# A hybrid decoder step: sample states streamed past C in four column groups, squares added ahead of their sums, diagonals in two instructions, the sample's list kept on the chip

## The chip, the cores and the metric

The kernel runs on one core of one Trainium2 chip. The metric is the device time of one execution in microseconds (us). A core has five engines that run at the same time, each through its own instructions in order: TensorE (PE in the profile, its weight loads PEld), VectorE (DVE), ScalarE (ACT), GpSimd (POOL) and SyncE (SP), whose queue issues most of the DMA transfers. They wait for one another by semaphores. TensorE reads SBUF and writes PSUM; the kernel takes PSUM in banks of 128 partitions x 512 f32 numbers.

## The reference, cut to what matters

One layer of a decoder step for 512 prompt tokens and 32 sample tokens (8 sequences of 4): a SwiGLU block, a mixing block with two parallel branches, attention over a memory, a second SwiGLU block. The change touches three places in the mixing block.

The state branch (SSD) has 8 groups of 4 heads, 64 channels a head, 128 state numbers a channel. For a group, `bm` and `cm` are its B and C (128 numbers a token), `xs` its input, and for the sample each sequence has a state `h0` of its own:

```
y_off = einsum('bctgn,bcgrpn->bctgrp', cc, h_in) * exp(a_cs)     # state times C
y = y_diag + y_off + d_skip * xs ;  y = y * silu(z)
yg = y by groups of 256 ;  yg = yg * rsqrt(mean(yg*yg) + EPS)     # norm of each group
```

The attention branch of the sample picks 256 of 4100 keys for each of the 32 tokens and attends to them alone:

```
score = sum over heads of wi * relu(qi . ki) ;  sel = top_k(score, 256)
phys = page_table[sel // 128] ; off = sel % 128      # keys and values come from paged pools,
                                                     # the last 4 positions are the new tokens
```

## The kernel before, in words

Activations lie transposed: features on partitions, 544 tokens (512 and 32) along the row. Each weight is split into a high and a low part (`wh`, made by ScalarE in L270, and `wl`, by VectorE in L271), each activation too (`uh`, `ul`), and the projections add three f32r products in L302; that line makes up most of TensorE's work. Weights come through SP's queue (L267) in pieces of 512 KB, with three raw and two split buffers.

Python generators issue the program. `weave` runs several at once: each yields an estimate of TensorE's time and of a delay, and `weave` takes the next one that is due. A scheduler of the language then orders each engine's instructions by its own estimate of when they are ready, so that an engine's order in the trace is near the order of issue but not the same; it also puts in all waits. A tile with a `tag` shares its buffers (`bufs`) with the other tiles of the tag, and a new tile waits until the old one's last reader is done.

In `ssd` two chains are woven with a third one as filler. `tails` runs `ssd_y` for the groups 0 to 7 one after another. The other chain is the sample's: the rest of `sample_lists`, then `sample_select`, then `sample_att`. The filler `fronts` runs the projections of the groups (`ssd_x`, `ssd_z`), up to two groups ahead of the tails, and when both are through the attention branch's output projection.

`ssd_y(g)`: the prompt's part is in chunks of 128 tokens (`pcb`, `pxt`, `pst`, later `pYo`, `pY`). For the sample, `turned(n)` transposes four sequences' states of two heads (L1395) and ScalarE copies them to `hT` (L1397, two buffers). Then four matmuls (L1409) each take one sequence's transposed state, 128x128, as the stationary operand and move that sequence's four columns of C (`XS[3]`) past it. This happens four times a group; results gather in the bank `pys`. L1414 adds the part of the new tokens to that bank, and L1417 (`pns`) makes the new states, which VectorE adds up (L1421) and SP stores (L1424). The decay E (L1439, one buffer) comes from DRAM in two halves (L1441) and multiplies the prompt's state part (L1454). `y` is formed for each of the group's two tiles, ScalarE squares it into `zts[i]` (L1463), and `rms` sums the squares over partitions: the squares are the stationary operand and a column of ones moves (L333), for both tiles and five blocks of tokens. After `rsqrt`, `rms` spreads the result over partitions: for each of the five blocks VectorE multiplies the identity by a column (L344, `dg`, two buffers) and TensorE multiplies ones by it (L345).

The sample's list: four partitions hold the four segments of a token's keys. `sample_lists` finds the threshold by bisection, numbers the selected keys of each segment by a running sum, and `max_index` (L1096) looks up the positions of the numbers 1 to 256 in each segment's own list. `sample_select` turns positions into rows of the pools (L1507 to L1517), counts which of the four new tokens are chosen (L1522), writes the four segment lists to DRAM (L1527), and reads them back shifted by the number of keys in the segments before (L1540), so that VectorE can put them together (L1544 to L1548). Two transposes and a copy give `slot` (L1552, L1553), the row numbers with which GpSimd gathers keys and values (L1591).

`sample_att` works in four steps of eight tokens. It spreads the queries into `qz` (16 small copies, L1601), adds two masks into the score bank `psS`: one (L1609) takes `lt`, which VectorE makes from the identity (L1608), and the list's mask `mk`, the other (L1610) takes `En`, loaded by SP (L1604, one buffer), and `bn`. Then the gathered keys are transposed (L1619), scored (L1626), and after the softmax the values are multiplied (L1663): 32 columns of weights are the stationary operand and 128 columns of values move, four of these matmuls going to the four 32-partition quarters of the bank `pO`.

Of the kernel before, what the change touches and what calls it, by code (L numbers as in the profile page):

```python
# [17 lines left out]
P = 128  # L18
# [12 lines left out]
def consts():  # L31
# [41 lines left out]
    less = seg[:, None] < a(4)[None]  # L73
    start = ((p // 4 * 16 + p % 4)[:, None] + a(4)[None] * 4) * 256
    c["c_ix2"] = f(np.concatenate([nm, same, Pre, it256, onb, onq, less, start], 1))
# [7 lines left out]
    c["c_att"] = f(np.concatenate([hm, En.reshape(P, 512)], 1))  # L83
# [85 lines left out]
class Net:  # L169
# [155 lines left out]
    def rms(self, sqs, inv_n, pool):  # L325
# [14 lines left out]
        yield 0.3, 4.0  # L340
        ps = self.ps1("psr")
# [366 lines left out]
    def mix(self, lead):  # L708
# [7 lines left out]
        self.mk = mx.tile([32, 256], F32, name="mk")  # L716
# [317 lines left out]
    def sample_lists(self):  # L1034
# [3 lines left out]
        ct = sp.tile([P, 560], F32, name="ct")  # L1038
        nc.sync.dma_start(ct, I["c_ix2"][:, 4:])
        cx = self.cx = views(ct, (("Blk", P), ("Pre", P), ("it256", 256), ("onb", 8), ("onq", 32), ("less", 4), ("start", 4)))  # L1040
        bits = sp.tile([P, 16, 3], U32, name="bits")
        nc.sync.dma_start(bits.rearrange("p a b -> p (a b)"), I["c_bits"])
        w = sp.tile([P, 24], F32, name="selw")
# [48 lines left out]
        nc.vector.scalar_tensor_tensor(A, S, n, A, op0=ALU.is_le, op1=ALU.mult)  # L1092
        nc.vector.tensor_tensor_scan(S, A, G, 0.0, op0=ALU.add, op1=ALU.add)
        yield 0.0, 3.0
        for r in range(32):
            nc.vector.max_index(self.IX[:, r * 8:(r + 1) * 8], cx["it256"][:, r * 8:(r + 1) * 8], S)  # L1096
            yield 0.0, 2.6
# [119 lines left out]
    def ssd(self, sel_ex, rounds):  # L1217
# [4 lines left out]
        self.fr, self.zt = {}, {}  # L1222
        fs = Flag()
# [83 lines left out]
    def ssd_y(self, g, z):  # L1307
# [65 lines left out]
        yield 0.5, 5.0  # L1373

# [12 lines left out]

        yield 0.0, 2.0
        ys = self.ps1("pys")
# [10 lines left out]
        turned(0)  # L1400
        yield 0.45, 0.8
        for n in range(4):
            i, q = n // 2, n % 2
            if n < 3:
                turned(n + 1)
                yield 0.45, 0.8
# [3 lines left out]
            yield 0.1  # L1410
# [24 lines left out]
        sqs = []  # L1435
        Y = []
        for i in range(2):
# [26 lines left out]
            sqs.append(zts[i])  # L1464
            Y.append(y)
        yield 0.0, 8.0
# [25 lines left out]
    def sample_select(self):  # L1492
        nc, I = self.nc, self.I
        IX, cx, c = self.IX, self.cx, self.cnt
        ex = ExitStack()
        sp = self.pool("sel", ex)
        dum = sp.tile([P, 256], F32, name="dum")

# [4 lines left out]
        nc.vector.tensor_scalar(ptf, ptb, 128.0, None, op0=ALU.mult)  # L1503
        pgi = sp.tile([P, 256], U32, name="pgi")
# [11 lines left out]
        nc.vector.tensor_scalar(dum, pgf, 8.0, 65536.0, op0=ALU.is_equal, op1=ALU.mult)  # L1516
        nc.vector.tensor_tensor(row, row, dum, op=ALU.add)  # L1517
        sel = sp.tile([P, 256], F32, name="selm")
        nc.vector.tensor_scalar(sel, cx["it256"], c, None, op0=ALU.is_le)
        fl = sp.tile([P, 4], F32, name="fl")  # L1520
        for j in range(4):
            nc.vector.scalar_tensor_tensor(dum, row, 65536.0 + j, sel, op0=ALU.is_equal, op1=ALU.mult, accum_out=fl[:, j:j + 1])  # L1522
        bn = self.bn
# [27 lines left out]
        for hf in range(2):  # L1551
            nc.tensor.transpose(ps[:, hf * 32:(hf + 1) * 32], R[:, 1, hf * P:(hf + 1) * P], self.ident[:32, :32])  # L1552
# [506 lines left out]
```

## Time and profile before

| what | value |
|---|---|
| median of 3 runs | 2251.27 us (2251.18 to 2252.69) |
| profiled execution, its own time | 2257.89 us |
| its span | 2256.1 us |
| mean granted TensorE clock over the span | 0.976 |
| TensorE busy | 2135.5 us, 95% |
| VectorE busy | 1336.8 us, 59% |
| ScalarE busy | 937.7 us, 42% |
| GpSimd busy | 475.9 us, 21% |

Busy time is the time in which an engine had at least one instruction of its own under way. Matmuls overlap in the pipeline, so a record's own length is more than what it costs; the distance from one start to the next tells that better. The granted clock has two levels in these records, 1.00 (2.4 GHz) and 0.50 (1.2 GHz). Each f32 matmul leaves two records, each f32r matmul one.

### The profile page before, as it was taken

The numbers are of one execution on the slowest core, as the hardware profiler recorded it, in microseconds if no ns is written. First come the engines' busy times: TensorE is split into PE (matmuls) and PEld (weight loads), VectorE is DVE, ScalarE is ACT, GpSimd is POOL, SyncE is SP. The second block draws the span as 40 slices with busy tenths as digits, with TensorE's granted clock in tenths as the row PEclk, the third lists the DMA queues.
The fourth block names the chain that finished last, engine by engine and source line by source line (L and its number), as shares of the span: only waits on it lengthen the run. The fifth ranks groups of instructions, "written<-read, shape, count | busy, mean of one in ns | idle before, by whom it ended". The sixth has DMA issues, their size and how long they took to land.

```text
span 2256.1 us, 41414 instructions
## 1 busy us (share of the span) xinstructions
PE 2135.5 (95%) x16769; PEld 2000.0 (89%) x16769; DVE 1336.8 (59%) x2801; ACT 937.7 (42%) x1717; POOL 475.9 (21%) x553
## 2 busy tenths in 40 slices
PE   7999999998999999879999999999999979999998
PEld 7999999997787689878888899999897879999998
DVE  6543333484778898885676578554664385423445
ACT  6323354355436664343444345232435253222233
POOL 0000010142132212245654531012420140000012
PEclk9999999999999999998999999999999999999999
DMA  6324564457432243255465454473444434232243
GB/s 204 113 80 141 164 214 164 128 133 228 143 94 84 72 114 113 70 159 146 140 178 152 121 145 153 139 226 99 161 150 143 171 99 131 79 99 87 87 122 104
DMA packets 319803, 301.72 MB, mean 134 GB/s; under 512 B 25432, under 2 KB 290264, under 8 KB 318564
## 3 DMA queue, kind: packets, MB, share of 16 engines
q1 hardware_dynamic: 310076, 272.45, 39.6%
q0 software_dynamic: 8576, 25.31, 3.7%
q8 instruction: 132, 2.16, 0.4%
q10 hardware_dynamic: 960, 1.31, 0.2%
q14 instruction: 59, 0.48, 0.1%
HBM read 261.01 MB, written 37.48 MB: 132 GB/s over the span
## 4 chain that ended last, share of the span: by engine, by line
PE 70%; DVE 14%; ACT 5%; POOL 4%; DMA 4%; issue 4%; SPq 0%; another core or an unknown queue 0%; DVEq 0%; POOLq 0%; ACTq 0%
PE pg L302 40%; PE pgh L302 14%; PE pmo L580 2%; DVE wl L271 2%; ACT wh L270 2%; DVE gtm L1065 1%; DVE XO L1297 1%; POOL kv L1591 1%; PE pys L1409 1%; DVE eqm L1096 1%; DMA wr<-in_ffn_wu 1%; POOL hT L375 1%; DMA yt<-yssd_d 1%; PE pmo L1852 1%; PE pkT L1619 1%
## 5 line engine op out<-in xcount | busy, mean ns | idle before, releaser
L270 ACT CAST wh<-wr 128x1024 fp32r<-128x1024 f32 (+3 forms) x362 | 341.0, 958 | 506.5 <-PE pg L302 278.6
L302 PE MATMUL pg<-uh,wh 128*128 128x256 f32 (+1 forms) x2336 | 506.7, 298 | 3.3 <-ACT CB L1285 1.5
L271 DVE TENSOR_TENSOR wl<-wr,wh 128x1024 fp32r<-128x1024 f32 (+3 forms) x338 | 390.2, 1167 | 199.4 <-ACT wh L270 191.1
L302 PE MATMUL pg<-uh,wl 128*128 128x256 f32 (+1 forms) x2336 | 496.0, 293 | 5.7 <-DVE wl L271 5.7
L302 PE MATMUL pg<-ul,wh 128*128 128x256 f32 (+1 forms) x2336 | 495.1, 293 | 0.0
L302 PEld LDWEIGHTS pg<-uh,wh 128*128 128x128 f32 x2336 | 383.1, 192 | 23.2 <-issue 16.7
L302 PEld LDWEIGHTS pg<-uh,wl 128*128 128x128 f32 x2336 | 382.5, 192 | 8.6 <-DVE wl L271 6.2
L302 PEld LDWEIGHTS pg<-ul,wh 128*128 128x128 f32 x2336 | 383.1, 192 | 2.9 <-issue 2.1
L302 PE MATMUL pgh<-uh,wl 128*128 128x256 f32 (+1 forms) x880 | 258.3, 296 | 12.2 <-DVE wl L271 11.8
L302 PE MATMUL pgh<-uh,wh 128*128 128x256 f32 (+2 forms) x880 | 260.9, 299 | 6.7 <-ACT wh L270 4.6
L302 PE MATMUL pgh<-ul,wh 128*128 128x256 f32 (+2 forms) x880 | 257.5, 294 | 1.9 <-POOL ul L311 1.2
L302 PEld LDWEIGHTS pgh<-uh,wl 128*128 128x128 f32 x880 | 168.5, 192 | 16.7 <-DVE wl L271 15.3
L302 PEld LDWEIGHTS pgh<-uh,wh 128*128 128x128 f32 (+1 forms) x880 | 170.0, 194 | 10.6 <-ACT wh L270 5.5
L302 PEld LDWEIGHTS pgh<-ul,wh 128*128 128x128 f32 (+1 forms) x880 | 170.7, 194 | 4.3 <-POOL ul L311 1.6
L359 POOL TENSOR_TENSOR sqf<-sqf,sqt 128x256 f32<-128x256 f32 (+1 forms) x52 | 55.8, 1073 | 516.7 <-ACT sqt L358 516.6
L302 PE MATMUL pgh<-hh,wh 128*128 128x288 f32 (+1 forms) x352 | 101.7, 289 | 0.0
L302 PE MATMUL pgh<-hh,wl 128*128 128x288 f32 (+1 forms) x352 | 100.9, 287 | 0.0
L302 PE MATMUL pgh<-hl,wh 128*128 128x288 f32 (+1 forms) x352 | 100.9, 287 | 0.0
L691 POOL DMA_INDIRECT G<-in_cache_kidx,ix x16 | 16.4, 1027 | 361.6 <-DVE ix L686 280.2
L1297 DVE SCALAR_TENSOR_TENSOR XO<-CB,convw,XO 128x600 f32<-128x600 f32 x96 | 80.3, 837 | 18.3 <-ACT XO L1295 17.8
L606 DVE TENSOR_TENSOR g<-pg,rt 128x544 f32<-128x544 f32 x32 | 23.2, 725 | 102.2 <-PE pg L302 102.2
L609 DVE TENSOR_TENSOR g<-pg,g 128x544 f32<-128x544 f32 x32 | 23.2, 725 | 99.3 <-PE pg L302 99.3
(605 smaller groups left out, 3965.3 us busy)
## 6 DMA issues: line engine op xcount, KB each, us to landing
wr<-in_w_in SPq DMA_DIRECT2D x66, 512.0 KB
wr<-in_ffn_wg SPq DMA_DIRECT2D x48, 512.0 KB
wr<-in_ffn_wu SPq DMA_DIRECT2D x48, 512.0 KB
wr<-in_ffn_wd SPq DMA_DIRECT2D x44, 384.0 KB
wr<-in_ffn_wd SPq DMA_DIRECT2D x44, 320.0 KB
kt_d<-KT SPq DMA_DIRECT2D x8, 1024.0 KB
KT<-kt_d SPq DMA_DIRECT2D x16, 512.0 KB
wr<-in_w_in SPq DMA_DIRECT2D x32, 256.0 KB
```

The lines of the kernel that those rows point to most:

```text
L270: nc.scalar.copy(hi[:, s], r)
L271: (lo_eng or nc.vector).tensor_tensor(lo[:, s], r, hi[:, s].bitcast(F32), op=ALU.subtract)
L302: nc.tensor.matmul(o, a[:, k, c0:c0 + m], x[:, r0:r0 + n], start=(k == 0 and j == 0), stop=(k == KT - 1 and j == 2))
L359: (nc.vector if last else nc.gpsimd).tensor_tensor(acc[:, :n], acc[:, :n], s[:, :n], op=ALU.add)
L375: (nc.gpsimd if k % 2 else nc.vector).tensor_tensor(hT[:, k, sl], hT[:, k, sl], y[:, k, sl], op=ALU.add)
L580: nc.tensor.matmul(ps[:, :256], a[:, k, i * P:(i + 1) * P], b[:, k, :], start=(k == 0 and j == 0), stop=(k == 7 and j == 2))
L606: nc.vector.tensor_tensor(g1[:, :n], pg, rt[:, sl], op=ALU.mult)
L609: nc.vector.tensor_tensor(g1[:, :n], pu, g1[:, :n], op=ALU.mult)
L1065: nc.vector.scalar_tensor_tensor(G, S, thr[:, j:j + 1], one, op0=ALU.is_ge, op1=ALU.mult, accum_out=cnt[:, j:j + 1])
L1096: nc.vector.max_index(self.IX[:, r * 8:(r + 1) * 8], cx["it256"][:, r * 8:(r + 1) * 8], S)
L1297: nc.vector.scalar_tensor_tensor(xo, CB[:, j:j + 600], cw(j), xo, op0=ALU.mult, op1=ALU.add)
L1409: nc.tensor.matmul(ys[:, i * 64 + b * 4:i * 64 + b * 4 + 4], hTs[n][:, b4, :], XS[3][:, b * 4:b * 4 + 4], start=True, stop=True)
```

## The change

In `ssd_y`, C becomes the stationary operand. GpSimd makes CZ, zeros with each sequence's four columns of C in a block of its own 32 columns (a step of 36 moves them four columns on in each block), in E's buffer. Two blocks of states are turned, then two bursts of four matmuls run; each matmul moves 128 columns of one state block past 32 columns of CZ and writes one 32-partition quarter of the bank, and sequences that share a quarter add up there. ScalarE copies the two 128x128 results to `yr`, and for each a matmul with `r32` (four small identities under one another) adds the quarters and turns the result back. VectorE adds the two tiles of squares, so that `rms` gets one tile. In `rms` all four full diagonals are made by one instruction, the small one by a second, and two matmuls spread them.

In the list, a matmul (`Pre`) counts the keys in the segments before, the searched numbers are shifted by that count before the search, so that each segment's list stands at its final place, and one matmul over all partitions puts the four together. The trip through DRAM goes. The counts of the new tokens come from the last four columns of the selection. In `sample_att` the queries are spread by 8 copies, `lt` is loaded from a constant by SP, and `mk` has 128 partitions.

```diff
@@ rms
-        for i, (c0, n) in enumerate(blk):
-            dg = pool.tile([P, P], F32, tag="dg", name="dg", bufs=2)
-            nc.vector.tensor_scalar(dg[:n, :n], self.ident[:n, :n], y[:n, i:i + 1], None, op0=ALU.mult)
-            nc.tensor.matmul(ps[:, c0:c0 + n] if i < 4 else st[:, 64:96], self.ones[:n, :], dg[:n, :n], start=True, stop=True)
+        nc.vector.tensor_tensor(sq[:, :TP].rearrange("p (i c) -> p i c", i=4), self.ident.unsqueeze(1).broadcast_to([P, 4, P]),
+                                y[:, :4].unsqueeze(2).broadcast_to([P, 4, P]), op=ALU.mult)
+        nc.vector.tensor_scalar(sq[:32, TP:], self.ident[:32, :32], y[:32, 4:], None, op0=ALU.mult)
+        nc.tensor.matmul(ps, self.ones, sq[:, :TP], start=True, stop=True)
+        nc.tensor.matmul(st[:, 64:96], self.ones[:32, :], sq[:32, TP:], start=True, stop=True)
@@ sample_lists, ahead of the search
+        fl = w[:, 22:26]
+        nc.vector.tensor_tensor(fl, A[:, 1024:], G[:, 1024:], op=ALU.add)
...
+        nc.tensor.matmul(ps[:, 0:1], cx["Pre"], c, start=True, stop=True)
+        yield 0.2, 3.0
+        bg = w[:, 26:27]
+        nc.vector.tensor_copy(bg, ps[:, 0:1])
+        at = self.at = cx["it256"]
+        nc.vector.tensor_scalar(at, at, bg, None, op0=ALU.subtract)
@@ ssd_y
+        CZ = sp.tile([P, 384], F32, tag="E", name="CZ")[:, :288]
+        nc.gpsimd.memset(CZ, 0.0)
+        nc.gpsimd.tensor_copy(CZ.rearrange("p (b x) -> p b x", x=36)[:, :, :4], XS[3].rearrange("p (b t) -> p b t", b=8))
...
-                nc.tensor.matmul(ys[:, i * 64 + b * 4:i * 64 + b * 4 + 4], hTs[n][:, b4, :], XS[3][:, b * 4:b * 4 + 4], start=True, stop=True)
+                nc.tensor.matmul(pt[b4 * 32:(b4 + 1) * 32, i * P:(i + 1) * P], CZ[:, b * 32:(b + 1) * 32], hTs[n][:, b4, :],
+                                 start=(q == 0), stop=(q == 1))
+
+        turned(0)
+        turned(1)
+        yield 0.9, 1.6
+        burst(0)
+        burst(1)
+        turned(2)
+        turned(3)
+        yield 1.4, 1.6
+        burst(2)
+        burst(3)
+        yr = sp.tile([P, 4, P], F32, tag="hT_", name="yr", bufs=2)[:, :2]
+        nc.scalar.copy(yr.rearrange("p a b -> p (a b)"), pt[:, :256])
+        yield 0.5, 1.2
+        for i in range(2):
+            nc.tensor.matmul(ys[:, i * 64:i * 64 + 32], yr[:, i, :], self.r32, start=True, stop=True)
...
-            sqs.append(zts[i])
+        nc.vector.tensor_tensor(zts[0], zts[0], zts[1], op=ALU.add)
+        sqs = zts[:1]
+        yield 0.0, 9.0
@@ sample_select
-        lst = self.dr.tile([P, 256], F32, name="lst")
-        nc.sync.dma_start(lst, row)
...
-        for s in range(4):
-            nc.gpsimd.indirect_dma_start(out=R[:, s, :], out_offset=None, in_=lst,
-                                         in_offset=bass.IndirectOffsetOnAxis(ap=bi[:, s:s + 1], axis=1))
-        yield 0.1, 9.0
...
+        nc.vector.tensor_scalar(own, at, 0.5, None, op0=ALU.is_gt)
+        nc.vector.scalar_tensor_tensor(own, at, c, own, op0=ALU.is_le, op1=ALU.mult)
+        nc.vector.scalar_tensor_tensor(self.mk, pgf, 8.0, own, op0=ALU.is_equal, op1=ALU.mult)
+        nc.vector.tensor_tensor(own, own, self.mk, op=ALU.subtract)
+        nc.vector.tensor_tensor(row, row, own, op=ALU.mult)
+        nc.vector.tensor_scalar(self.mk, self.mk, NEG, None, op0=ALU.mult)
...
-            nc.tensor.transpose(ps[:, hf * 32:(hf + 1) * 32], R[:, 1, hf * P:(hf + 1) * P], self.ident[:32, :32])
+            nc.tensor.matmul(ps[:, hf * 32:(hf + 1) * 32], row[:, hf * P:(hf + 1) * P], cx["onq"], start=True, stop=True)
@@ sample_att
-                nc.vector.tensor_copy(lt[:, gp], self.ident[:32, st * 8:st * 8 + 8].unsqueeze(2).broadcast_to([32, 8, 8]))
+            lt = sp.tile([P, P], F32, tag="lt", name="lt")
+            nc.sync.dma_start(lt, I["c_att"][:, 514 + st * P:514 + (st + 1) * P])
```

## Rows read from the trace of the kernel before

**Rows 1.** The page: busy time and share of the span; the chain by engine.
```profile
PE 2135.5 (95%) x16769; PEld 2000.0 (89%) x16769; DVE 1336.8 (59%) x2801; ACT 937.7 (42%) x1717; POOL 475.9 (21%) x553
...
PE 70%; DVE 14%; ACT 5%; POOL 4%; DMA 4%; issue 4%; SPq 0%; another core or an unknown queue 0%; DVEq 0%; POOLq 0%; ACTq 0%
```

**Rows 2.** Windows: the stage of the change and two parts of it, in us.
```profile
core 0: us, PE busy (x) PEld busy (x) DVE busy (x) ACT busy (x) POOL busy (x), PEclk, DMA share, GB/s
850.00:1450.00 600.00, 555.57 (x4459) 509.57 (x4459) 424.90 (x990) 254.79 (x476) 234.65 (x329) 0.95 0.47 137
920.00:1060.00 140.00, 117.28 (x864) 106.54 (x863) 101.09 (x260) 48.97 (x91) 53.57 (x67) 0.90 0.43 129
1340.00:1450.00 110.00, 108.45 (x858) 103.67 (x859) 75.97 (x176) 48.26 (x89) 9.99 (x22) 0.95 0.47 140
```

**Rows 3.** Order of time, TensorE, two runs of L1409: start, us, instruction, [idle before].
```profile
1204.81 0.95 PE L1409 MATMUL pys<-XS,hT__13007 128*128 128x4 f32 x8
1205.62 1.03 PE L1409 MATMUL pys<-XS,hT__13040 128*128 128x4 f32 x8
1206.58 0.30 PE L1414 MATMUL pys<-Gs,xds 32*64 32x32 f32 x4
```

**Rows 4.** Order of time, TensorE, a run of L1663 between projections.
```profile
1068.10 0.41 PE L302 MATMUL pg<-uh,wl 128*128 128x256 f32 x2
1068.44 0.64 PE L1663 MATMUL pO<-kv,PZ 128*32 128x128 f32 x16
1069.01 0.52 PE L302 MATMUL pg<-uh,wh 128*128 128x256 f32 x2
1069.37 0.41 PE L302 MATMUL pg<-ul,wh 128*128 128x256 f32 x2
```

**Rows 5.** Order of time, TensorE, a run of L333.
```profile
1433.19 2.06 PE L333 MATMUL st<-ones,zt 128*128 128x1 f32 x20
1435.18 0.52 PE L302 MATMUL pg<-uh,wh 128*128 128x256 f32 x2
```

**Rows 6.** Groups of VectorE by line and shape: busy us, mean ns | idle before.
```profile
L606 DVE TENSOR_TENSOR g<-pg,rt 128x544 f32<-128x544 f32 x32 | 23.2, 725 | 102.2 <-PE pg L302 102.2
...
L344 DVE TENSOR_SCALAR dg<-ident,nw 128x128 f32<-128x128 f32 x32 | 8.1, 284 | 5.0 <-PE psr L345 4.8
L1322 DVE TENSOR_TENSOR cb<-pcb,tri 128x512 f32<-128x512 f32 x8 | 5.5, 688 | 8.2 <-PE pcb L1320 5.6 <-issue 2.6
```

**Rows 7.** Windows with the granted clock at 0.50, columns as in rows 2.
```profile
1207.90:1211.30 3.40, 3.40 (x17) 3.30 (x16) 2.56 (x9) 0.57 (x1) 0.00 (x0) 0.50 0.01 2
...
1436.60:1440.00 3.40, 3.40 (x17) 3.40 (x16) 1.24 (x7) 0.00 (x0) 0.00 (x0) 0.50 0.03 11
1013.30:1020.10 6.80, 6.32 (x26) 5.67 (x27) 4.15 (x9) 0.59 (x1) 5.72 (x9) 0.50 0.37 108
```

**Rows 8.** TensorE's waits, 850 to 1450 us: us in total, times, longest.
```profile
PE psr L345 <- DVE dg L344: 10.0, 3, 6.2
...
PE psS L1609 <- DVE lt L1608: 5.4, 1, 5.4
...
PE pslot L1552 <- DVE R L1548: 1.5, 1, 1.5
```

**Rows 9.** Order of time, VectorE: first and last instruction of `sample_select`.
```profile
957.49 0.15 DVE L1503 TENSOR_SCALAR ptf<-ptb 128x8 f32<-128x8 int32 x1
...
1004.35 0.23 DVE L1553 CAST slot<-pslot 128x64 int32<-128x64 f32 x1 [0.40 <-PE pslot L1552]
```

**Rows 10.** Waits of SP's queue, 850 to 1450 us.
```profile
SPq L1424 <- DVE h L1421: 102.9, 8, 32.0
...
SPq L1604 <- PE psS L1610: 16.2, 2, 13.8
```

**Rows 11.** Groups of TensorE over the whole span, the bisection's line.
```profile
L1068 PE MATMUL pbis<-selw,ct 128*128 128x3 f32 x32 | 5.5, 243 | 4.0 <-DVE gtm L1065 2.8 <-ACT PT L1194 0.9 <-DVE st L1168 0.2
```

**Rows 12.** VectorE's waits, 850 to 1450 us.
```profile
DVE E L1454 <- DMA E<-ac_d: 14.3, 6, 6.4
```

More of the change, by code (lines that the diff above doesn't have):

```diff
@@ L72, in consts @@
     onq = (bb[:, None] * 4 + tt[:, None]) == a(32)[None]
-    less = seg[:, None] < a(4)[None]
-    start = ((p // 4 * 16 + p % 4)[:, None] + a(4)[None] * 4) * 256
-    c["c_ix2"] = f(np.concatenate([nm, same, Pre, it256, onb, onq, less, start], 1))
+    c["c_ix2"] = f(np.concatenate([nm, same, Pre, it256, onb, onq], 1))
     hm = (p[:, None] % 8) // 4 == a(2)[None]
@@ L1037, in sample_lists @@
         sp = self.sb
-        ct = sp.tile([P, 560], F32, name="ct")
+        ct = sp.tile([P, 552], F32, name="ct")
         nc.sync.dma_start(ct, I["c_ix2"][:, 4:])
-        cx = self.cx = views(ct, (("Blk", P), ("Pre", P), ("it256", 256), ("onb", 8), ("onq", 32), ("less", 4), ("start", 4)))
+        cx = self.cx = views(ct, (("Blk", P), ("Pre", P), ("it256", 256), ("onb", 8), ("onq", 32)))
         bits = sp.tile([P, 16, 3], U32, name="bits")
         nc.sync.dma_start(bits.rearrange("p a b -> p (a b)"), I["c_bits"])
-        w = sp.tile([P, 24], F32, name="selw")
+        w = sp.tile([P, 28], F32, name="selw")
         wu = w.bitcast(U32)
@@ L1222, in ssd @@
         self.fr, self.zt = {}, {}
+        self.r32 = self.sp.tile([P, 32], F32, name="r32")
+        for q in range(4):
+            nc.vector.tensor_copy(self.r32[q * 32:(q + 1) * 32], self.ident[q * 32:(q + 1) * 32, q * 32:(q + 1) * 32])
         fs = Flag()
@@ L1388, in ssd_y @@
         yield 0.0, 2.0
-        ys = self.ps1("pys")
+        pt = self.ps1("pys")
+        ys = pt[:, 256:]
         hTs = []
@@ L1398, in turned, with burst @@
             hTs.append(hT)
-        turned(0)
-        yield 0.45, 0.8
-        for n in range(4):
+        def burst(n):
             i, q = n // 2, n % 2
-            if n < 3:
-                turned(n + 1)
-                yield 0.45, 0.8
             for b4 in range(4):
                 b = q * 4 + b4
-                nc.tensor.matmul(ys[:, i * 64 + b * 4:i * 64 + b * 4 + 4], hTs[n][:, b4, :], XS[3][:, b * 4:b * 4 + 4], start=True, stop=True)
-            yield 0.1
+                nc.tensor.matmul(pt[b4 * 32:(b4 + 1) * 32, i * P:(i + 1) * P], CZ[:, b * 32:(b + 1) * 32], hTs[n][:, b4, :],
[15 more added lines that the diff above has]
+            nc.tensor.matmul(ys[:, i * 64:i * 64 + 32], yr[:, i, :], self.r32, start=True, stop=True)
         for i in range(2):
@@ L1434, in ssd_y @@
         zts = self.zt[g]
-        sqs = []
         Y = []
@@ L1514, in sample_select @@
             yield 0.0, 0.9
[L1516 to L1522, printed above, removed]
@@ L1605, in sample_att @@
             psS = self.ps1("psS")
-            lt = sp.tile([32, 2, 8, 8], F32, tag="lt", name="lt")
-            for gp in range(2):
-                nc.vector.tensor_copy(lt[:, gp], self.ident[:32, st * 8:st * 8 + 8].unsqueeze(2).broadcast_to([32, 8, 8]))
-            nc.tensor.matmul(psS[:, :256], lt.rearrange("p a b c -> p (a b c)"), self.mk, start=True, stop=False)
+            lt = sp.tile([P, P], F32, tag="lt", name="lt")
+            nc.sync.dma_start(lt, I["c_att"][:, 514 + st * P:514 + (st + 1) * P])
+            nc.tensor.matmul(psS[:, :256], lt, self.mk, start=True, stop=False)
             nc.tensor.matmul(psS[:, 256:288], En, self.bn.rearrange("p b j -> p (b j)"), start=False, stop=False)
@@ L1625, in scores @@
                         q8 = order[n + z]
-                        nc.tensor.matmul(psS[rg(gp, q8), :288], cols(qz[:, gp], q8), KTs[z][:, gp, :], start=False, stop=(n == 6))
+                        nc.tensor.matmul(psS[rg(gp, q8), :288], qcols(qz[:, gp], q8), KTs[z][:, gp, :], start=False, stop=(n == 6))
             for n in range(0, 8, 2):
```

53 lines of the change are left out of this document (20 added, 33 removed).

## The prediction

> **What bounds the kernel now.** The page comes first. TensorE is busy for 95% of the span and holds 70% of the chain that ended last; VectorE is busy for 59% [rows 1]. So I count TensorE's time, and ask of every other engine only whether it makes TensorE wait. Everything the diff touches on TensorE lies between 850 and 1450 us, where the eight groups of `ssd_y` run beside the sample's selection and attention; the windows say how full that is [rows 2]. Of 600 us TensorE is busy 555.6, so 44 us are waits. They are not spread evenly: 22.7 lie in 920 to 1060 us, where the sample's list is made and its attention starts, and only 1.6 in 1340 to 1450 us. The granted clock is 0.95 over the stage. What shortens TensorE's own instructions here should shorten the kernel, as long as the places with waits do not take it back.
>
> **The states streamed past C.** Before, each transposed block of states is the stationary operand and four columns of C move past it. In the order of time one run of four such matmuls (eight records, since each f32 matmul leaves two) takes 0.81 us until the next work starts, and one of the last pair until L1414 0.96; 1.77 for the two [rows 3]. I take 0.84 for each of the 32 runs (eight groups, four each): 26.9 us. After, C is the stationary operand, 32 columns wide, the states move, 128 columns, and four matmuls go to four groups of columns. The trace holds the very same form, in L1663 of the sample's attention. Sixteen such records start at 1068.44 and the projection goes on at 1069.01: 0.57 us for eight matmuls, that is for two of the new bursts. The way in and out of the narrow form costs more: the two projection records of 1068.10 would have been followed at 1068.35, and after the run the projection's next row comes 0.36 us later instead of 0.25 [rows 4]. Between 0.57 and 0.77 I take 0.7 for each of the 16 pairs: 11.2 us, 15.7 less.
>
> The result then has to be turned back: per group one ScalarE copy of 128x256, and two matmuls with a 128x128 stationary operand, four records. The run of 20 full loads in L333 lasts 1.99 us, 0.1 each [rows 5], so 0.4 a group and 3.2 in all. Net: **-12.5 us**.
>
> **Squares.** The two tiles of squares are added on VectorE, and L333 issues 10 records a group instead of 20: 80 records of 0.1 [rows 5], **-8.0 us**. The add of 128x544 costs VectorE 0.73 by the like of L606 [rows 6], 5.8 us over eight groups. VectorE has 175 us free in the stage [rows 2]; if that cover were gone, the 5.8 would stand on the path.
>
> A record of L333 moves one column and takes 0.1 us by its start-to-start time [rows 5]. The Trainium skill (TensorEngine Tiling (Array Packing), Instruction Overhead) gives a matmul of one column the cost of one of 60, about 60 cycles; at 2.4 GHz that is an estimate of 25 ns, by which the 80 records would save 2.0 us instead of 8.0 and the sum come to 2228. The row is four times that, so the trace does not agree for f32 runs with full loads, and I keep the row.
>
> **Diagonals.** Five small multiplies of 0.28 us and five matmuls become one multiply of 128x512 (0.69 by L1322), one of 32x32 and two matmuls [rows 6]. The same number of columns goes through TensorE, so I cost it at nothing, between -2 (fewer starts) and +2 us: the first matmul now waits for 0.7 us of VectorE and not for 0.28, and three times in the stage TensorE already stood there, 10.0 us in all [rows 8]. That wait is VectorE's lateness in the chain before it, which stays.
>
> **The clock.** Nine stretches of 3.4 us in this stage were granted 0.50, that is 1.2 instead of 2.4 GHz (at 904.1, 1047.5, 1163.5, 1207.9, 1279.6, 1286.4, 1354.7, 1378.6 and 1436.6 us; two of them are shown), with TensorE busy all the time [rows 7]. Each came after a run that the change shortens: 1207.9 after the 16 records of L1409 [rows 3], 1436.6 after the 20 of L333 [rows 5]; five of the nine followed L1409 and four L333. Half clock for 3.4 us loses 1.7, so they cost 15.3 us. L1409's narrow form goes, L333's run is halved, but not every such run was followed by a drop, and the new transposes stand closer together. I take six of nine: **-10.2 us**, between 0 and -15.3.
>
> **The sample's list.** Gone: the trip through DRAM, four gathers, nine operations on R and the four counts; new: six short operations on 128x256. In the trace the section runs from 957.49 to 1004.35 us [rows 9]. That is latency beside other work, and at its end TensorE still has the projection to do, so finishing it about 20 us earlier moves the sample's attention forward but shortens no TensorE work: nothing by itself. Two waits hang on it. `pslot` waited 1.5, and the first `psS` 5.4 for `lt`, which VectorE built behind its copies [rows 8]; afterwards the clock was 0.50 for 6.8 us [rows 7], 3.4 more. Now `lt` comes by a transfer on SP's queue, behind En's. SP already stands up to 13.8 us there until the last En was read [rows 10]; lt's buffer is free one matmul sooner, so what is queued behind, weights above all, waits no longer than before. Whether the 8.8 us come back depends on what is late next: the gathered keys cannot be there before the slots are known. I take half, **-4.4**, bounds 0 and -8.8. The matmul for `Pre` is moved ahead of the search; TensorE may wait for VectorE's counts there, as `pbis` did, 2.8 us over 32 records [rows 11]: 0 to 2.8.
>
> **What is new to wait for.** CZ lies in E's buffer. Before, SP fetched the next group's first E as soon as the old one was read, far ahead. Now that transfer cannot go before the group's last burst, and behind it on SP's queue stand the stores and the weights; behind E's first reader on VectorE stand the low parts of the weights. VectorE waited for E 14.3 us in all, six times, the longest 6.4 [rows 12]. Twice as many exposed fetches would be another 14.3 us on VectorE; with 175 us free there I put a third on TensorE, 4.8. For the copies of yr on ScalarE, CZ on GpSimd behind the gathers and `Pre` I add 1.2. **+6 us**; bounds 0 and, were the longest wait paid in each group and handed on in full, 51.
>
> **Sum.** -12.5 - 8.0 + 0 - 10.2 - 4.4 + 6 = -29.1 us. The profiled execution took 2257.89 us, which gives 2228.8; the median of the runs is 6.6 lower, 2251.27, which gives **2222 us**.
>
> **Rivals.**
> *The clock does not come back.* The low stretches came with TensorE busy throughout [rows 7], after runs that move few columns, and the change leaves such runs: transposes now stand eight together around each pair of bursts, and half of L333. If the drops only find other places, and the wait for `lt` becomes one for the gathered keys, there remain -12.5 - 8.0 + 6 = -14.5: 2237 us. For it: 1279.6 and 1286.4 fell among such mixed work. Against it: 1207.9 and 1436.6, each with one long narrow run before it. Chance 0.25. The Trainium skill (TensorE: Matmul & The Clock Gate, Part 4: PE-mode transpose) states that transposes do not count as work for the clock in the way other matmuls do, which would bring this rival about; no run here has shown it yet.
>
> *New waits eat the gain.* Four to five us of waiting in each of the eight groups cancel the 35.1 us of the other terms: about 2251 us, no change within 0.2% (4.5 us, about what a measurement of this kernel can tell from none). For it: the stage's own 44 us of waits, and E. Against it: 1340 to 1450 us, where the last two groups run with hardly a wait. Chance 0.08.
>
> *E late: slower.* One mechanism: E's transfer, held until the last burst, lands late in every group, VectorE stops in front of it with the weights' low parts behind, and TensorE follows. At 6.4 us in each of eight groups it is +51.2 - 35.1 = +16 us, 2267 us; it decides from 4.4 us a group on. For it: six waits for E already [rows 12], and SP's queue holds stores that wait 103 us for VectorE [rows 10]. Against it: VectorE has time free, and the projection's matmuls fill TensorE meanwhile. Chance 0.06.
>
> *All of it comes.* No drop, no wait for `lt`, no new wait: -12.5 - 8.0 - 15.3 - 8.8 = -44.6, 2207 us. Chance of coming below 2212: 0.12.
>
> **How the numbers follow.** My forecast, 2212 to 2231, has 0.49. Faster by more than 0.2%: 0.49 + 0.12 + 0.25 = 0.86; same 0.08; slower 0.06. The range for eight in ten goes from the best case, 2207, to the clock rival with its new waits doubled, 2243; above it lie the 0.14 and a little of that rival, below it a little of the best case.
>
> **What would show it.** Right: L1409's new line at about 11 us of starts instead of 27, sixteen records in 0.6 to 0.8 us; 80 records in L333; fewer than four of the nine low stretches; no wait of `psS` for `lt`. Wrong: a granted clock of 0.95 or less over the stage with its place moved; VectorE's wait for E over 40 us; TensorE waiting in the bursts for hT, yr or CZ; or an idle share in 920 to 1060 us no smaller than now.

## The result, and the profile after

Before and changed kernel ran in turn on one chip, four times each: 2251.22 us before (2248.29 to 2252.69), **2222.28 us** after (2219.80 to 2226.15). The ratio is 0.9874, with a 95% interval of 0.9858 to 0.9890: 28.4 us faster, 24.8 to 32.0. The profiled execution after took 2223.0 us (span 2221.2, mean granted clock 0.977), 34.9 less than the profiled one before. The two traces run alike up to 820 us; from 850 us to the first matmuls of the branches' merge the changed one is 33.2 us shorter, so the gain lies in the stage that the change touches. Run again later, beside some of the experiments, it gave 0.9896 (0.9876 to 0.9915), 23.4 us; the mean of the two is about 26.

The page of the changed kernel, busy time by engine and the chain by engine, as [rows 1]:

```profile
PE 2106.5 (95%) x16675; PEld 1964.2 (88%) x16675; DVE 1327.6 (60%) x2733; ACT 939.9 (42%) x1725; POOL 471.6 (21%) x565
...
PE 68%; DVE 15%; DMA 5%; ACT 5%; issue 4%; POOL 3%; SPq 0%; DVEq 0%; POOLq 0%; ACTq 0%
```

TensorE lost 29 us of busy time and kept its 95%: work went, and waiting did not grow. Its windows of time, in which the changed kernel is up to 33 us further on in its work, columns as in [rows 2]; the last three are stretches at half clock, as in [rows 7]:

```profile
850.00:1450.00 600.00, 560.18 (x4651) 507.60 (x4650) 434.52 (x938) 272.30 (x510) 233.76 (x343) 0.96 0.51 151
920.00:1060.00 140.00, 125.80 (x1042) 114.29 (x1041) 98.59 (x232) 51.05 (x98) 65.53 (x81) 0.94 0.53 159
1340.00:1450.00 110.00, 107.38 (x866) 101.33 (x865) 74.96 (x150) 47.81 (x85) 10.11 (x15) 1.00 0.61 190
1063.10:1069.90 6.80, 5.29 (x24) 5.29 (x25) 4.17 (x18) 4.10 (x11) 3.31 (x3) 0.50 0.88 260
977.70:987.90 10.20, 7.32 (x33) 7.03 (x34) 2.30 (x12) 2.92 (x7) 8.19 (x11) 0.50 0.52 155
1121.10:1127.90 6.80, 6.07 (x41) 4.62 (x41) 0.00 (x0) 1.06 (x2) 4.78 (x6) 0.50 0.48 153
```

From 1340 to 1450 us the clock was 0.95 before and is 1.00 now. The low stretches that are left look different: none of the three is filled with TensorE work as the first two of [rows 7] were. Four of the other five are filled, but right ahead of each of these TensorE waited 3.1 to 4.6 us. The new stream itself, in TensorE's order of time (start, us, instruction), answers to [rows 3]:

```profile
1262.82 0.41 PE L302 MATMUL pg<-uh,wl 128*128 128x256 f32 x2
1263.15 0.43 PE L1427 MATMUL pys<-hT__13845,CZ 128*32 128x128 f32 x8
1263.40 0.40 PE L1427 MATMUL pys<-hT__13852,CZ 128*32 128x128 f32 x8
1263.73 0.43 PE L1664 MATMUL pO<-vs,PN 32*64 32x128 f32 x4
```

Two bursts go from 1263.15 to 1263.73, 0.58 us, where two runs of L1409 took 1.77. From each start to the next matmul's, the 256 records took 26.84 us before and take 10.54, and yr's 32 records (L1444) 3.65. TensorE's waits from 850 to 1450 us (us in total, times, longest), as [rows 8]:

```profile
PE st L333 <- DVE zt L1498: 7.1, 3, 3.6
PE pg L302 <- DVE wl L271: 7.0, 2, 5.7
PE pcb L1338 <- DVE XO L1318: 6.6, 4, 4.6
PE pkT L1627 <- DMA kv<-in_cache_k,slot: 5.8, 5, 2.8
PE psr L347 <- DVE zt L344: 5.5, 2, 3.9
PE pO L1671 <- DMA kv<-in_cache_v,slot: 3.8, 2, 3.0
```

All its waits here add up to 39.5 us; before, 44.5. (The 44.5 are of that kernel's one profile, which is longer than its runs are; more on this with the experiments.) The wait for `lt` is gone and that for the diagonals has halved; st now waits for the added squares, and pkT and pO for gathered keys and values. What stands behind the first of these is in the order of time around 1060 us, first TensorE, then VectorE:

```profile
1058.96 0.41 PE L302 MATMUL pg<-uh,wl 128*128 128x256 f32 x2
1059.21 0.41 PE L302 MATMUL pg<-uh,wh 128*128 128x256 f32 x2
...
1059.97 1.04 PE L1627 MATMUL pkT<-ident,kv 128*128 128x128 f32 x8
1064.61 2.03 PE L333 MATMUL st<-ones,zt 128*128 128x1 f32 x10 [3.61 <-DVE zt L1498]
...
1067.19 0.66 PE L302 MATMUL pg<-ul,wh 128*128 128x256 f32 x2
1067.65 0.66 PE L302 MATMUL pg<-uh,wl 128*128 128x256 f32 x2
...
1058.70 0.56 DVE L1487 TENSOR_TENSOR E<-pYo,E 128x384 f32<-128x384 f32 x1 [6.19 <-DMA E<-ac_d]
...
1060.91 1.16 DVE L1495 SCALAR_TENSOR_TENSOR y<-y,zt 128x544 f32<-128x544 f32 x1
...
1063.75 0.72 DVE L1498 TENSOR_TENSOR zt<-zt,zt 128x544 f32<-128x544 f32 x1
```

VectorE stood 6.19 us in front of E; y, its square and the addition came late in turn, TensorE stood 3.61 us, and from 1063.1 its clock was 0.50 for 6.8 us, in which the ten records of st took 1.97 us start to start. The projection's two records take 0.46 us from start to start there (1067.19 to 1067.65), against 0.25 at full clock (1058.96 to 1059.21). VectorE's waits for E and the new one of SP's queue, 850 to 1450 us, answer to [rows 10, 12]:

```profile
DVE E L1487 <- DMA E<-ac_d: 15.8, 5, 6.2
...
SPq L1474 <- PE pys L1427: 42.9, 8, 14.6
```

SP does hold each group's first E until the last burst, 42.9 us in all, but VectorE's wait for E went only from 14.3 to 15.8.

### The profile page after: what moved, and what is told of

The parts are those of the page before. It is cut to its first block, busy times and chain, and to the rows that moved or that the text cites. A ratio compares the mean times of both kernels' runs of the same rounds, so it can differ in the third digit from the quotient of the medians.

```text
span 2221.2 us, 41234 instructions
## 1 busy us (share of the span) xinstructions
PE 2106.5 (95%) x16675; PEld 1964.2 (88%) x16675; DVE 1327.6 (60%) x2733; ACT 939.9 (42%) x1725; POOL 471.6 (21%) x565
## 4 chain that ended last, share of the span: by engine, by line
PE 68%; DVE 15%; DMA 5%; ACT 5%; issue 4%; POOL 3%; SPq 0%; DVEq 0%; POOLq 0%; ACTq 0%
PE pg L302 39%; PE pgh L302 15%; DVE wl L271 2%; PE pmo L583 2%; ACT wh L270 2%; DVE XO L1315 2%; DVE gtm L1068 1%; DVE eqm L1111 1%; POOL kv L1601 1%; DMA abc<-ac_d 1%; DMA yt<-yssd_d 1%; POOL hT L378 1%; DMA wr<-in_ffn_wu 1%; PE pmo L1860 1%; PE pmkT L1794 1%
## 5 line engine op out<-in xcount | busy, mean ns | idle before, releaser
L302 PEld LDWEIGHTS pg<-uh,wh 128*128 128x128 f32 x2336 | 381.1, 191 | 22.8 <-issue 19.4
L302 PE MATMUL pgh<-uh,wl 128*128 128x256 f32 (+1 forms) x880 | 258.4, 296 | 13.3 <-DVE wl L271 13.1
L302 PEld LDWEIGHTS pgh<-uh,wh 128*128 128x128 f32 (+1 forms) x880 | 169.3, 193 | 10.6 <-ACT wh L270 5.6
```

Source lines behind the costliest of these rows:

```text
L302: nc.tensor.matmul(o, a[:, k, c0:c0 + m], x[:, r0:r0 + n], start=(k == 0 and j == 0), stop=(k == KT - 1 and j == 2))
```

## The experiments

Twelve kernels, on three chips; each is set against the kernel before on the same chip. Each run lists its span and the mean granted clock of the span. If a stretch at 0.50 lost half its length, (1 - mean clock) x span would be what the low clock cost: for the kernel before 2246.8 x (1 - 0.9747) = 57 us over 16 runs on the first chip. The last two columns split the difference of the mean spans into this cost and the rest (streaming and waits). With the spread of the clock from run to run (0.0003 to 0.0012 as the standard error of a kernel's mean) the clock's column has a standard error of 2 to 3 us.

The split gives the clock too much. Full of projection rows, a stretch loses 0.45 of its length (0.46 us for 0.25 us of work, above) and not 0.5, and where TensorE stands in front of another engine's work, as from 1063.1 to 1064.61 us, it loses nothing by the clock. The runs say the same: among the runs of one kernel on one chip, a microsecond more of (1 - mean clock) x span comes with 0.73 us more of span (130 runs, 95% interval 0.64 to 0.82). By this, about a quarter of a number in the clock's column belongs to the rest.

The split also shows that the one profile of the kernel before is not a typical run. Its rest is 0.976 x 2256.1 = 2202 us, where the 47 runs of this kernel beside the experiments have 2190 to 2192 on average and at most 2197. So a wait of this profile set against a wait of another can differ by some microseconds for no reason of the change; the other profiles lie within 6 us of their kernels' means.

| kernel | median us (runs) | ratio, 95% interval | clock | rest |
|---|---|---|---|---|
| changed, again | 2225.43 (6) | 0.9896, 0.9876 to 0.9915 | -2.4 | -20.5 |
| bursts undone | 2244.01 (11) | 0.9976, 0.9961 to 0.9991 | +2.4 | -7.4 |
| squares undone | 2230.64 (6) | 0.9906, 0.9885 to 0.9927 | -0.1 | -19.2 |
| list undone | 2230.39 (6) | 0.9909, 0.9880 to 0.9938 | -10.5 | -8.2 |
| bursts alone | 2224.48 (6) | 0.9894, 0.9875 to 0.9914 | -8.1 | -15.7 |
| CZ in its own buffer | 2224.12 (6) | 0.9897, 0.9878 to 0.9915 | -1.8 | -22.3 |
| diagonals undone | 2219.89 (5) | 0.9881, 0.9861 to 0.9901 | -7.3 | -21.2 |
| norm later | 2221.26 (5) | 0.9885, 0.9865 to 0.9904 | -8.1 | -17.1 |
| narrow, new order | 2240.98 (7) | 0.9962, 0.9947 to 0.9976 | +8.4 | -15.5 |
| list alone | 2255.10 (12) | 1.0031, 1.0012 to 1.0050 | +8.9 | -2.0 |
| squares alone | 2237.80 (8) | 0.9953, 0.9937 to 0.9969 | -1.0 | -8.0 |
| diagonals undone, norm later | 2224.07 (5) | 0.9893, 0.9875 to 0.9910 | -4.3 | -20.3 |

**The changed kernel again**, beside the three that undo a part of it.

> The changed kernel once more, beside the three that undo one part of it each, so that all four are read on one chip: 2222 us, 2219 to 2226, ratio 0.987.

Measured 2225.43, ratio 0.9896: the time inside, the ratio a little above. Its trace has the same waits (st 8.7, pkT 5.8 us) at the same places. Only 2.4 of its 23 us are clock.

**The bursts undone.**

```diff
-        CZ = sp.tile([P, 384], F32, tag="E", name="CZ")[:, :288]
...
-                nc.tensor.matmul(pt[b4 * 32:(b4 + 1) * 32, i * P:(i + 1) * P], CZ[:, b * 32:(b + 1) * 32], hTs[n][:, b4, :],
-                                 start=(q == 0), stop=(q == 1))
+                nc.tensor.matmul(ys[:, i * 64 + b * 4:i * 64 + b * 4 + 4], hTs[n][:, b4, :], XS[3][:, b * 4:b * 4 + 4], start=True, stop=True)
```

> The changed kernel with the old stream of C past the sample states (32 narrow matmuls a group, four columns each, sums straight into their place; no zeroed CZ, no yr, no r32). Theory: the streaming returns (26.8 us start to start against 10.5 + 3.7, so +12.6) and with it the 0.50 stretches of 3.4 us right after the narrow runs of L1409 (five to seven of the nine, 1.7 us each, +8.5 to +12): 2241 to 2247, and the trace shows such stretches again right behind L1409. Rival: the clock falls for what stands before and behind, whichever way C is streamed; then only the streaming returns: 2233 to 2236. Second rival: the new waits (CZ in E's buffer) had taken most of it: 2225 to 2230.

Measured 2244.01: 18.6 us more than the changed kernel on that chip, in the theory's range. The rest is 13.1 us longer (20.5 less 7.4), and the streaming in the trace 13.4 (27.66 against 10.57 + 3.65): the term is all there. The clock adds 4.8 us. But only two of the eleven low stretches between 830 and 1500 us came right behind a narrow run; eight had a wait of TensorE of 1.9 us or more at their start, and one, at 831.9 us, had neither. So the size was as expected, the place mostly not.

**The narrow form in the new order.** As above, but the order of the changed kernel is kept: two states turned, then their 16 narrow matmuls, twice.

```diff
-                nc.tensor.matmul(pt[b4 * 32:(b4 + 1) * 32, i * P:(i + 1) * P], CZ[:, b * 32:(b + 1) * 32], hTs[n][:, b4, :],
-                                 start=(q == 0), stop=(q == 1))
+                nc.tensor.matmul(ys[:, i * 64 + b * 4:i * 64 + b * 4 + 4], hTs[n][:, b4, :], XS[3][:, b * 4:b * 4 + 4], start=True, stop=True)
...
-        yr = sp.tile([P, 4, P], F32, tag="hT_", name="yr", bufs=2)[:, :2]
```

> The changed kernel with the narrow matmuls of before in the place of the bursts, but in the new order (two turned states, then their 16 narrow matmuls, twice), and no CZ, yr, r32: the form of the stream alone, apart from its order. Theory: the form decides: 13.4 us of streaming and the clock of the narrow runs come back as with the whole part undone: 2238 to 2248. Rival: the order (two states turned together, their copies hidden by other work) brought what the part was worth above its streaming: 2232 to 2237.

Measured 2240.98, ratio 0.9962, its interval overlapping that of the bursts undone: the theory, the form decides. By the split the new order made the rest 8.1 us shorter than the old one and the clock 6.0 dearer; nothing that can be told is left of it.

**The bursts alone**, put into the kernel before.

> The kernel before with the stream of C changed alone (CZ, bursts on four column groups, yr, r32); squares, diagonals and list as before. Undoing this part alone cost 18.6 us on the last chip (13.4 of streaming, the rest in the clock: 27 us more at 0.50). Theory: the streaming is sure and the clock's share depends on the order that comes out; ratio to the kernel before 0.990 to 0.995, that is 12 to 22 us faster, and streaming of 13 us less in the trace. Rival: the parts only work together (without the shorter psr and lt waits the later start brings nothing): under 8 us faster.

Measured ratio 0.9894, that is 23.9 us (19.4 to 28.1): a little over the theory's range, and no sign that the parts need each other. This one part is nearly the whole gain: 15.7 of streaming and waits and 8.1 of clock. In its profiled execution TensorE's waits from 850 to 1450 us are 26.5 us, against 44.5 in the profile before. Over the runs the waits fell by much less: the rest of 15.7 us, less the 12.9 of streaming that the trace shows (26.84 against 10.18 + 3.76), leaves 2.8. The largest waits:

```profile
PE psr L345 <- DVE dg L344: 6.2, 3, 3.8
PE pg L302 <- DVE wl L271: 4.6, 1, 4.6
PE st L333 <- ACT zt L1482: 4.1, 4, 2.4
```

**The squares undone.**

```diff
-        nc.vector.tensor_tensor(zts[0], zts[0], zts[1], op=ALU.add)
-        sqs = zts[:1]
-        yield 0.0, 9.0
+        sqs = zts[:2]
+        yield 0.0, 8.0
```

> The changed kernel with the two tiles of squares summed by the matmuls again (two matmuls a column instead of one, no VectorE addition ahead of st; the yield ahead of them 8.0 as before). Theory: st had become 7.3 us shorter and had got a wait of 7.1 us for the addition, with two low-clock stretches of 6.8 us behind it; but the addition only names who is late: VectorE stood in front of E's DMA, and the second tile of squares comes just as late without it. So the wait stays within 1 to 2 us a group at the two places, and 4 to 7 us of streaming come back: 2226 to 2229. Rival: the addition itself is the wait; without it the 7.1 us and the 6.8 us of clock (two stretches, half of 13.6) go and the streaming of 7.3 returns, with drops after narrow runs at st: 2217 to 2222.

Measured 2230.64, 5.2 us more than the changed kernel on that chip: the 4 to 7 us of the theory, though the time is above its 2226 to 2229 and the intervals of the two ratios overlap. At the two places where st waited for the addition, 3.6 and 3.1 us, it now waits 1.7 and 2.1 for other work, and the clock is at 0.50 for 6.8 us from 1065.1 and for 10.2 from 1225.5 all the same. The addition was not the cause of these drops.

**The squares alone**, in the kernel before.

> The kernel before with the squares of a group added on VectorE ahead of st, alone (yield 9.0 for 8.0). Theory: st's streaming halves (7.3 us) and about half of it is given to the wait for the addition: 2 to 6 us faster than the kernel before (ratio 0.997 to 0.999). Rival: the drops of the clock behind narrow st runs go as well: 8 to 12 us faster (0.995).

Measured ratio 0.9953, 10.6 us (7.0 to 14.2), in the rival's range, but not by its reason: by the split 8.0 are rest and only 1.0 is clock. st's starts fell from 17.87 us, 1.4 of them its wait, to 9.52, and the addition was waited for 3.7 us. Of the runs of 18 and 20 records with which the kernel before gets its sums, the clock dropped right behind 10 of 28, counted over the four profiles that have them and leaving out the runs that already ran at half clock; behind the runs of ten it dropped after 9 of 70. (Right behind means within 3.5 us of the start of a run's last record, here and below.) The drops behind the narrow runs of C stay: here is one, at the same place as in [rows 3], in the order of time, and under it the window behind it, columns as in [rows 2].

```profile
1205.41 0.95 PE L1409 MATMUL pys<-XS,hT__13025 128*128 128x4 f32 x8
1206.22 1.03 PE L1409 MATMUL pys<-XS,hT__13067 128*128 128x4 f32 x8
1207.19 0.30 PE L1414 MATMUL pys<-Gs,xds 32*64 32x32 f32 x4
```

```profile
1208.00:1211.40 3.40, 3.40 (x17) 3.30 (x16) 2.36 (x10) 0.00 (x0) 0.00 (x0) 0.51 0.02 5
```

**The diagonals undone**: five small multiplies and five matmuls a group again, in the changed kernel.

```diff
-        nc.tensor.matmul(ps, self.ones, sq[:, :TP], start=True, stop=True)
-        nc.tensor.matmul(st[:, 64:96], self.ones[:32, :], sq[:32, TP:], start=True, stop=True)
+        for i, (c0, n) in enumerate(blk):
+            dg = pool.tile([P, P], F32, tag="dg", name="dg", bufs=2)
```

> The changed kernel with the five diagonals and five matmuls of the norm again, one VectorE instruction and one matmul a block. Theory: psr and st streaming is 10.06 against 10.41 us, and the wait for the diagonal 5.5 against 10.0, so the part is worth 2 to 5 us: 2226 to 2230. Rival: the waits only move (the first matmul starts earlier with one block's diagonal than with four): 2219 to 2225.

Measured 2219.89, ratio 0.9881, between the two ratios of the changed kernel: the rival, the part is worth nothing that can be told (its rest differs by 0.7 us). psr waits 4.0 us for the first diagonal and streams 10.36 us, against 5.5 and 10.06 with two instructions.

**The list undone** in the changed kernel, and **the list alone** in the kernel before.

```diff
-        nc.vector.tensor_scalar(at, at, bg, None, op0=ALU.subtract)
...
+        lst = self.dr.tile([P, 256], F32, name="lst")
+        nc.sync.dma_start(lst, row)
...
+            nc.tensor.transpose(ps[:, hf * 32:(hf + 1) * 32], R[:, 1, hf * P:(hf + 1) * P], self.ident[:32, :32])
```

> The changed kernel with the sample's list made as before (shifted through DRAM by gathers, mask of 32 rows, lt made on VectorE). Theory: the wait of psS for lt (5.4 us) comes back with its clock, but the waits of pkT for the gathers of kv (5.8 us, then 10.2 us at half clock) get shorter, since the later start covered them: 2222 to 2226. Rival: the list is worth its whole 8.8 us, since the gathers' wait was there anyway: 2229 to 2232. Second rival: the order of the parts moves only, and the list is worth nothing: 2221 to 2223.

> The kernel before with the sample's list changed alone. Theory: the wait for lt (5.4 us) and its clock go, and the gathers of kv, which it had covered, are waited for in their place: 0 to 4 us faster than the kernel before (ratio 0.998 to 1.000). Rival: worth its 8.8 us (ratio 0.996).

Undone, 2230.39, with runs from 2221 to 2239: a time inside the rival's range; but it is 5 us more than the changed kernel on that chip, less than the 7 to 10 that the rival stood for, with intervals that overlap. Alone, ratio 1.0031: **7.0 us slower** (2.7 to 11.3), which neither theory had. By the split the list costs 8.1 us of clock in the changed kernel (10.5 less 2.4) and 8.9 alone, against 12.3 and 2.0 us that it gives back in streaming and waits. With 0.73 for the clock it is 6 us of clock both times, against some 10 and nothing; the standard error of each is 2 to 3 us. In the profile of the list alone the stretches at 0.50 between 830 and 1500 us add up to 75.1 us, before to 61.4. TensorE's waits there, 850 to 1450 us; its order of time from 964 us, TensorE first, then VectorE and ScalarE; and the window behind that, columns as in [rows 2]:

```profile
PE st L333 <- ACT zt L1475: 9.3, 4, 3.9
PE pcb L1332 <- DVE XO L1312: 9.1, 3, 7.5
PE st L333 <- DVE yas L1662: 4.2, 2, 2.6
```

```profile
964.74 0.42 PE L302 MATMUL pg<-ul,wh 128*128 128x256 f32 x2
969.05 0.58 PE L333 MATMUL st<-ones,zt 128*128 128x1 f32 x2 [3.89 <-ACT zt L1475]
972.73 3.45 PE L333 MATMUL st<-ones,zt 128*128 128x1 f32 x18 [3.09 <-ACT zt L1475]
976.11 0.82 PE L302 MATMUL pg<-uh,wl 128*128 128x256 f32 x2
```

```profile
964.09 0.72 DVE L1474 SCALAR_TENSOR_TENSOR y<-y,zt 128x544 f32<-128x544 f32 x1
...
968.04 0.40 ACT L1357 ACTIVATE abc<-abc,acs 128x128 f32<-128x128 f32 x1 [3.71 <-DMA abc<-ac_d]
968.35 0.64 ACT L1475 ACTIVATE zt<-y 128x544 f32<-128x544 f32 x1
```

```profile
967.70:981.40 13.70, 9.26 (x43) 9.14 (x44) 12.35 (x38) 9.04 (x21) 0.00 (x0) 0.50 0.81 236
```

The wait for `lt` is gone, and the slots are ready at 988.8 us instead of 1004.35 [rows 9]. But here TensorE stands twice, 7.0 us, in front of st for the squares of a group, with 13.7 us at half clock from 967.7 on. The kernel before waited at this place too, 4.4 us for a weight's low part, and had 6.8 us at half clock from 965.6. The first of the two waits is ScalarE's order: y was ready at 964.81, but ScalarE stood 3.71 us in front of the transfer for `abc` and squared y only behind it, at 968.35; in the kernel before, the square came ahead of `abc`, at 963.52. For the second, VectorE put the list's operations between those that make y and waited 2.0 us for E (before, 1.6), and the second square came at 972.03 instead of 969.79. One such place is 3.4 us of the clock's 8.9. In the whole stage TensorE waits 13.5 us for st here and 1.4 before, and four of the twelve stretches at 0.50, 30.7 of the 75.1 us, begin at or shortly behind such a wait; the other places were not followed one by one.

**CZ in a buffer of its own**, so that E need not wait for the bursts.

```diff
-        CZ = sp.tile([P, 384], F32, tag="E", name="CZ")[:, :288]
+        CZ = sp.tile([P, 288], F32, tag="CZ", name="CZ")
```

> The changed kernel with CZ in a buffer of its own instead of E's, so that E's DMA no longer has to wait for the bursts and CZ's zeroing no longer for the last read of E. Theory (the step priced at 4.8 us): SyncE's wait at E for the bursts (42.9 us, 8 times) and GpSimd's at CZ (23.9 us) go, and VectorE's wait for E (15.8) falls; as the kernel before waited 14.3 us there without the sharing, PE gains little: 2219 to 2226. Rival: E is what makes VectorE late before st; with E early, st's wait (7.1 us) and the two 6.8 us stretches at 0.50 behind it go: 2208 to 2215.

Measured 2224.12, ratio 0.9897: no difference. SP's wait for the bursts is gone and its stores wait 67.0 instead of 32.8 us for VectorE's new states; VectorE waits for E as before:

```profile
SPq L1458 <- DVE h L1455: 67.0, 8, 22.2
...
DVE E L1487 <- DMA E<-ac_d: 15.0, 5, 6.2
```

So the sharing cost nothing that can be told. st's wait is 6.5 against 7.1 us. The rival is not settled by this: E came no earlier with CZ out of its buffer, so what an early E would do for st is not shown.

**The norm later.**

```diff
-        yield 0.0, 9.0
+        yield 0.0, 13.0
         r, rs = yield from self.rms(sqs, 1.0 / 256, sp)
```

> The changed kernel with the time given to VectorE ahead of the norm's first matmuls (st) raised from 9 to 13 us, so that other work of TensorE stands before them. Theory: st's wait for the added squares (7.1 to 8.7 us in three places) goes and the low-clock stretches behind two of them: 8 to 12 us faster than the changed kernel where nothing waits for the later norm: 2211 to 2218. Rival: the later norm ends the stage later or pushes the wait to the next part: 2221 to 2228.

Measured 2221.26, ratio 0.9885: the rival. The wait for the added squares is no longer among the twelve largest, but others of 2 to 3 us stand in its place (st's last diagonal 3.3, pkT for ScalarE's copy 2.7, pst 2.1): by the split 5.7 us of clock are won and 3.4 of the rest lost, with nothing left that can be told.

**Diagonals undone and norm later together**, meant to beat the changed kernel.

> A version meant to beat the changed kernel: the diagonals one block at a time as before, and 13 us instead of 9 for VectorE ahead of the norm's matmuls. Theory: each was 1 to 3 us faster than the changed kernel's mean by itself, within the spread of the runs; together 2214 to 2221, ratio 0.986 to 0.988. Rival: neither does anything that can be told: 2220 to 2226.

Measured 2224.07, ratio 0.9893: the rival. No version was found that can be told from the changed kernel on the faster side.

## Why the prediction was right

**The sum.** Forecast -29.1 us, measured -28.4 and -23.4. Alone, the bursts give -23.9, the squares -10.6 and the list +7.0, and undoing the diagonals changes nothing: together -27.5, so the parts depend little on one another in time. Split, they are -0.2 of clock and -25.7 of rest, the whole, run again, -2.4 and -20.5. Sorted by kind, the forecast is -20.5 of streaming, -11.9 of clock (the list's half of 3.4 included) and +3.3 of waits. The whole, run again, has -18.8 of streaming in the trace (12.65 of C, 5.8 of st, 0.35 of the diagonals), -2.4 of clock and, from the rest of 20.5, -1.7 of waits, good to 2 or 3 us. The time was right; the clock and the waits inside it were not, their errors have opposite signs, and that the total fell within 1 us of the first measurement is luck.

**The states streamed past C: right.** The streaming term was -12.5 and measured -12.65 (26.84 against 10.54 + 3.65). A pair of bursts took 0.66 on the mean instead of 0.7, yr 3.65 instead of 3.2. Undoing it added 13.1 us of rest.

**The clock: the mechanism right for the part, the term for the whole too large.** All nine stretches that the prediction named are gone; one of them, at 1279.6 us, had TensorE waiting 0.58 us right ahead, and each lost nearer 1.5 than 1.7 us. In the five profiles with the narrow stream, a stretch at 0.50 began right behind 21 of 133 runs of its matmuls (a run counts if it was not at half clock already; the 21 share 15 stretches); in the nine with bursts, behind none of 169. A moment of the stage taken at random has such a start as close behind it in 7% of cases in the five and 5% in the nine. Bursts and squares alone won 8.1 and 1.0 us of clock, against the -10.2 of the step. But the whole won 2.4, because the list, by the split, gave 8 to 9 back (about 6 with the factor 0.73). The drops that are left stand behind waits: all eight in the changed kernel's stage, 47.8 us together, where before it was 34.0 of 61.4; by this pair of profiles the term is -6.8.

So the first rival, that the drops only find other places, had the clock's net nearly right, and missed the time because the rest gave 20.5 and not 14.5. In the nine profiles with bursts the clock dropped right behind 6 of 194 runs of the turned states, in the five others behind 6 of 144, no more often than at a random moment. The Trainium skill (TensorE: Matmul & The Clock Gate, Part 4: PE-mode transpose) states that transposes do not count as work for the clock in the way other matmuls do; these counts give that no support as the reason here. Of the 6 with bursts, five are one place, from 1110 to 1124 us, where TensorE also waits for gathers, 3.05 us in the changed kernel.

**Squares: right in size.** -8.0 forecast, -8.0 of rest alone; st's starts fell by 6.9 us without its wait. The Trainium skill (TensorEngine Tiling (Array Packing), Instruction Overhead) would have had 2.0: again the trace does not agree. In the changed kernel st's starts fell by 5.8, two of its runs being at half clock, and the addition is waited for 7.1 us in three places, as the prediction had priced it if VectorE's cover went; it went because VectorE stood in front of E, in a wait that was there before.

**Diagonals: right**, nothing.

**The list: the step that failed.** It put half of 8.8 us, -4.4, on the list, with 0 as its worst case, and asked only whether the gathered keys would be late next. They were (pkT 5.8 and pO 3.8 us in the changed kernel). What it left out is the clock, which the list made worse by 6 to 9 us, so that alone it costs 7.0: TensorE came to stand in front of st, 13.5 us instead of 1.4, and ran at half clock behind that. A step that moves work to another time on another engine had no ground for a bound at 0. Whether the list is worth anything in the whole change, 5 us by the medians, is not settled by the intervals.

**New waits: +6 forecast, nothing net.** 4.8 of it stood for E in CZ's buffer, and CZ in its own changed nothing. There were new waits, 16.7 us for the added squares and the gathers. Against them stand 9.9 less for `lt` and the diagonals and many small ones, in all 39.5 us in the stage instead of 44.5 in the profile before; over the runs the waits fell by the 1.7 us above. This error has the opposite sign of the clock's, and that is why the sum came out.

**What stays open.** Which of the waits draw a low stretch, and why the list alone or the new order of narrow matmuls drew more of them than the kernels beside them, was shown by sums over runs and one place, not by its cause. That st would wait less if E came earlier is likely from the order of time around 1060 us, but no run has it.

## What to carry to other kernels

Cost a matmul by the distance between starts in the trace, not by its columns: 32 runs with full loads and four columns cost TensorE nearly twice as much as bursts into four column groups with the turn back included (26.8 against 14.2 us), and the clock fell behind them besides. Split a difference into what the granted clock took and the rest before explaining it, over many runs, and test the split on the spread of one kernel: here a part gained next to nothing in work and lost 6 to 9 us of clock. See whether the profile compared with is a typical run. Undo each part, and also put each part alone into the kernel before: a part that costs 7 us alone stood in a change that gained 28, where taking it out made the kernel no faster.

## What the runs showed of the hardware

The same program does not get the same clock each time. In 20 runs of the kernel before on one chip the time went from 2241.4 to 2257.9 us, with mean granted clocks of the span between 0.972 and 0.979 (correlation of time and clock -0.9). That spread of 0.7% is larger than three of the four parts of this change.

The stretches at 0.50 lasted 3.4 us or longer (6.8, 10.2, 13.7, once 20.5), and began behind two kinds of places: with TensorE busy, behind narrow runs (8 of 15 in the stage before), and behind waits (all 8 after). In them the projection's two records take 0.46 us from start to start instead of 0.25. Which place drew one differed: of 23 runs of 16 narrow matmuls that were not at half clock already, 8 did.
